# A hybrid network on one core: the SSD stage without GpSimd, its 1/rms in two parts

## Chip, core, metric

One core of one Trainium2 chip runs the whole program: TensorE (PE), VectorE (DVE), ScalarE (ACT), GpSimd (POOL) and the DMA queues that SyncE (SP) feeds. The metric is the device time of one execution in microseconds; lower is better.

## What is computed

The network takes 512 tokens of width 1024 through a gated delta rule with a conv feed-forward, a chunked attention with another, an S5 mixer with a squared-ReLU MLP, a Mamba-2 mixer (SSD) with a second MLP, and a final norm. The change lies in the SSD mixer and in the first lines of the two MLPs. The reference of the mixer, cut:

```python
def _ssd_mixer(h, w_in, conv_w, conv_b, dt_bias, a_log, d, norm_g, w_out):
    z, xbc, dt_raw = jnp.split(h @ w_in, [M2_D_INNER, M2_D_INNER + M2_CONV_DIM], axis=-1)
    xbc = jax.nn.silu(_causal_dwconv(xbc, conv_w) + conv_b)
    xs, b_in, c_in = jnp.split(xbc, [M2_D_INNER, M2_D_INNER + G * N], axis=-1)
    ...
    y_diag = jnp.einsum('bcgls,bgrcls,bcsgrp->bclgrp', cb, l_mat, xdt)
    ...
    y = y_diag + y_off + xs * d.astype(f32).reshape(G, R, 1)
    y = y.reshape(bsz, L, M2_D_INNER) * jax.nn.silu(z.astype(f32))
    yg = y.reshape(bsz, L, G, M2_D_INNER // G)
    yg = yg * lax.rsqrt(jnp.mean(yg * yg, axis=-1, keepdims=True) + NORM_EPS)
    return (yg.reshape(bsz, L, M2_D_INNER) * norm_g).astype(h.dtype) @ w_out
# second_block: x = x + g1 * mixer(modulate(rmsnorm(x)))
```

The norm `yg` is taken over each of four groups of 512 channels, for every token.

## The kernel before

Features lie on the 128 partitions, the 512 tokens on the free axis. The residual is eight tiles `h` of 128x512. A product with a weight is made of three: weight and activation are each split into a high and a low part (`hi` by ACT at L305, `lo` by DVE at L306, activations in `split`), and `mm_ch` (L347 to L349) issues hi·hi, hi·lo and lo·hi. So a projection to 128 columns of the 1024 inputs is 24 matmuls, one from the 512 channels of a group 12. The PSUM banks are dealt out in lanes (`mm` for projections, `sm` for small products, `y`).

The mixer goes through its four groups. Written `I(g,i)`, group g has ten in-projections: 0 and 1 give B and C, 2 to 5 the four x tiles (these six get a causal convolution, three DVE operations at L607, and a SiLU), 6 to 9 the four gates z. `ssd_core(g, step)` is C0: the product C·B, masked, and B transposed; C1: x to token order and scaled (L1800, L1803), exp of the decay differences D, times C·B (L1835); C2 and C3: the chunk states and E's loads; C4 to C7: one y tile each, plus t, times z, split, squared and summed; C8: column sums (L1879), mean square (L1881), a Newton 1/sqrt on 128x4 (L420 to L427), a diagonal of it (`dg`, L1885), ones·dg (L1887) and the copy r (L1889). D of the next group is loaded from DRAM and 32 subtractions (L1757) made of it in C5 and C7. `O(g,i)`, the out-projections by pairs, are made from y without 1/rms; `ssd_out` multiplies by gate and r (L1895) and adds to `h` (L1898).

The order of the work is a list written out by hand in `ssd_seq`; a recording layer then interleaves what follows within each engine. C8 of a group stands behind I4 of the next:

```python
q += [I[4]] + ([("core", g - 1, 8)] if g else []) + [C[0], I[5], I[6], C[1]]
```

At the start of the stage four projections are already in PSUM (`heads`, made in `finish` of the stage before) and have to be multiplied by 1/rms of the input (`rb`, L1770) before their banks are free. `ssd_gates` follows (dt, its loads and small products). After the last group `finish` closes the next norm with L492.

POOL does the additions to `h` (27 of 32), the products D times C·B (28 of 32), and y plus t, y times z, the state decay and most sums of squares of the first three groups.

Of the kernel before, what the change touches and what calls it, by code (L numbers as in the profile page):

```python
# [224 lines left out]
class Net:  # L225
# [1359 lines left out]
    def mlp(self, l):  # L1585
# [3 lines left out]
        with ExitStack() as es:  # L1589
# [35 lines left out]
    def ssd(self, l):  # L1625
        nc = self.nc
        with ExitStack() as es:
            g1 = es.enter_context(self.tc.tile_pool(name="ssd1", bufs=1))
            wk = es.enter_context(self.tc.tile_pool(name="ssd", bufs=2))
            op = es.enter_context(self.tc.tile_pool(name="ssdo", bufs=6))  # L1630
            self.sg, self.swk, self.sop = g1, wk, op

# [9 lines left out]
            self.S = [dict(x={}, z={}, o={}, xd={}, prev={}) for _ in range(4)]  # L1642
            heads, self.heads = self.heads, None
            self.set_lanes(mm=(4, 0, 1, 2), sm=(3, 5, 6, 7))
            for name, g, i in self.ssd_seq():
                if name in ("in", "z") and heads:
                    self.ssd_in(g, i, heads.pop(0), self.shc["ssd"][:, i:i + 1])
                    if not heads:
                        self.ssd_gates()
                        self.set_lanes(mm=(0, 1, 2), sm=(3, 4, 5), y=(6, 7))  # L1650
                elif name == "in":
                    w = self.next("m2_in", 128)
                    ps = self.mmp()
                    self.mm_ch(ps, w, 0, self.xs())
                    self.ssd_in(g, i, ps)
                elif name == "out":
                    if (g, i) == (3, 0):
                        self.set_lanes(mm=(0, 1, 2, 6, 7), sm=(3, 4, 5))
                    w = self.next("m2_out", 256)
                    pss = [self.mmp() for _ in range(2)]  # L1660
                    for j in range(2):
                        self.mm_ch(pss[j], w, j * P, [self.S[g]["o"][k] for k in range(4)])
                    if (g, i) == (3, 0):
                        self.ssd_core(3, 8)
                    for j in range(2):
# [6 lines left out]
    sbufs = dict(x=5, z=4, xd=4, B=1, E=3, CB=1, Bt=1, prev=3, r=1)  # L1672

    def ssd_seq(self):

        q = [("in", 0, i) for i in range(4)]
        for g in range(4):
            I = [("in", g, i) for i in range(10)]
            N = [("in", g + 1, i) for i in range(4)]
            C = [("core", g, i) for i in range(9)]  # L1680
            O = [("out", g - 1, i) for i in range(4)]
            q += [I[4]] + ([("core", g - 1, 8)] if g else []) + [C[0], I[5], I[6], C[1]]
            if g == 0:
                q += [I[7], C[2], I[8], C[3], I[9], C[4], N[0], C[5], N[1], C[6], N[2], C[7], N[3]]
            elif g < 3:
                q += [I[7], C[2], O[0], C[3], I[8], O[1], C[4], I[9], N[0], C[5], O[2], N[1], O[3], C[6],
                      N[2], C[7], N[3]]
            else:
                q += [O[0], C[2], O[1], C[3], I[7], O[2], C[4], I[8], C[5], O[3], C[6], I[9], C[7]]
        return q + [("out", 3, i) for i in range(4)]  # L1690

    def ssd_plan(self):
        for name, g, i in self.ssd_seq():
            if name == "in":
                self.queue.append(("m2_in", 10 * g + i))
            elif name == "out":
                self.queue.append(("m2_out", 4 * g + i))
# [4 lines left out]
    def ssd_gates(self):  # L1702
# [42 lines left out]
        for hf in range(2):  # L1745
            self.ssd_rows(0, hf)

    def ssd_rows(self, g, hf):

        nc = self.nc  # L1750
        h0 = 8 * g + 4 * hf
        self.S[g]["D", hf] = d = self.stile("D", 4)
        nc.sync.dma_start(out=d, in_=self.srow[0, h0:h0 + 4, :].partition_broadcast(P))
        for r in range(4):
            for c in range(4):
                x = d[:, r, c * P:(c + 1) * P]
                nc.vector.tensor_scalar(out=x, in0=x, scalar1=self.acs[:, h0 + r, c:c + 1], scalar2=0.0,  # L1757
                                        op0=ALU.subtract, op1=ALU.min)

    def ssd_in(self, g, i, ps, shift=None):  # L1760
# [21 lines left out]
    def ssd_core(self, g, step):  # L1782
# [22 lines left out]
        def state(c):  # L1805
# [5 lines left out]
            else:  # L1811
                t = self.stile("t")
                gp.tensor_tensor(out=r3(t, 8), in0=r3(S["prev"][c], 8), in1=hb(self.decb, c), op=ALU.mult)
# [13 lines left out]
        elif step == 1:  # L1827
            to_tok(0)
            to_tok(1)
            for hf in range(2):  # L1830
                d = S["D", hf]
                s.activation(d, d, AF.Exp)
                for r in range(4):
                    e = v if g == 0 and r % 2 else gp
                    e.tensor_tensor(out=d[:, r, :], in0=d[:, r, :], in1=S["CB"], op=ALU.mult)  # L1835
# [13 lines left out]
        elif step < 8:  # L1849
# [9 lines left out]
            e = v if g == 3 else gp  # L1859
# [8 lines left out]
            if 0 < j < (3 if g == 3 else 4):  # L1868
                (v if j == 3 else e).tensor_tensor(out=sq, in0=S["sq"], in1=sq, op=ALU.add)
            S["sqs"], S["sq"] = ([S["sq"], sq] if (g, j) == (3, 3) else [sq]), sq  # L1870
            if j % 2 == 1 and g < 3:
                self.ssd_rows(g + 1, j // 2)
        else:

            ps = self.smp()
            sqs = S["sqs"]
            for c in range(4):
                for x in sqs:
                    pe.matmul(ps[:, c:c + 1], x[:, cs(c)], self.ones[:, 0:1], start=x is sqs[0], stop=x is sqs[-1])  # L1879
# [3 lines left out]
            dg = self.stile("t")  # L1883
# [3 lines left out]
            pe.matmul(ps, self.ones, dg, start=True, stop=True)  # L1887
            S["r"] = self.stile("r")
            s.copy(S["r"], ps)  # L1889

    def ssd_out(self, g, ot, ps, gate):

        nc = self.nc
        t = self.stile("t")
# [4 lines left out]
        if g == 3:  # L1899
            self.done(ot)  # L1900
# [150 lines left out]
```

## Time and profile before

| | us |
|---|---|
| median of 3 runs | 2775.3 (2773.09 to 2775.48) |
| the profiled execution, its own time | 2773.28 |
| its span in the profile | 2771.5 |
| the SSD stage, 1998.0 to 2404.5 | 406.5 |
| mean granted TensorE clock of the span | 0.982 |

The profile is one execution. Times in it run from the start of the span. A busy time is that of an engine's instructions; a wait is the idle time of an engine in front of an instruction with what released it; the granted clock is the share of TensorE's full speed that it was given in the stretch, where 1.0 stands for 2.4 GHz and 0.5 for 1.2 GHz.

### The profile page before, as it was taken

The numbers are of one execution on the slowest core, as the hardware profiler recorded it, in microseconds if no ns is written. First come the engines' busy times: TensorE is split into PE (matmuls) and PEld (weight loads), VectorE is DVE, ScalarE is ACT, GpSimd is POOL, SyncE is SP. The second block draws the span as 40 slices with busy tenths as digits, with TensorE's granted clock in tenths as the row PEclk, the third lists the DMA queues.
The fourth block names the chain that finished last, engine by engine and source line by source line (L and its number), as shares of the span: only waits on it lengthen the run. The fifth ranks groups of instructions, "written<-read, shape, count | busy, mean of one in ns | idle before, by whom it ended". The sixth has DMA issues, their size and how long they took to land. (4 is left out here: it accounts for less than half of the span.)

```text
span 2771.5 us, 36994 instructions
## 1 busy us (share of the span) xinstructions
PE 2638.3 (95%) x14002; PEld 2121.9 (77%) x14002; DVE 1932.4 (70%) x3332; ACT 1178.4 (43%) x1867; POOL 514.9 (19%) x448
## 2 busy tenths in 40 slices
PE   8899999999999999979998999999999898999998
PEld 6677778888786868767877778888767787778886
DVE  7878889797938689998577565444677767844343
ACT  7555454242437554234264352332554433533232
POOL 0211010000112210446642110000224333300001
PEclk9999999999999999989999999999999999999999
DMA  5323247676733335354449434333333332232322
GB/s 180 121 81 83 75 137 235 214 239 203 232 114 94 109 109 162 99 156 133 145 143 268 130 118 127 98 99 92 93 118 101 114 114 80 71 96 93 99 96 72
DMA packets 172706, 356.34 MB, mean 129 GB/s; under 512 B 44048, under 2 KB 81648, under 8 KB 171504
## 3 DMA queue, kind: packets, MB, share of 16 engines
q1 hardware_dynamic: 163056, 349.78, 40.3%
q10 hardware_dynamic: 9472, 4.20, 0.5%
q8 instruction: 110, 1.80, 0.3%
q14 instruction: 68, 0.56, 0.1%
HBM read 324.00 MB, written 25.72 MB: 126 GB/s over the span
## 5 line engine op out<-in xcount | busy, mean ns | idle before, releaser
L305 ACT CAST hi<-raw 128x1024 fp32r<-128x1024 f32 (+1 forms) x416 | 432.4, 1041 | 863.3 <-PE mm L348 750.2
L347 PE MATMUL mm<-xh,hi 128*128 128x512 f32 x1824 | 739.6, 406 | 23.7 <-ACT hi L305 10.5
L349 PE MATMUL mm<-xh,lo 128*128 128x512 f32 x1824 | 727.2, 399 | 1.1 <-DVE lo L306 1.1
L348 PE MATMUL mm<-xl,hi 128*128 128x512 f32 x1824 | 724.1, 397 | 0.8 <-DVE xl L441 0.8
L306 DVE TENSOR_TENSOR lo<-raw,hi 128x1024 fp32r<-128x1024 f32 (+1 forms) x416 | 529.8, 1274 | 250.8 <-ACT hi L305 243.4
L347 PEld LDWEIGHTS mm<-xh,hi 128*128 128x128 f32 x1824 | 348.5, 191 | 103.3 <-ACT hi L305 14.6
L349 PEld LDWEIGHTS mm<-xh,lo 128*128 128x128 f32 x1824 | 347.2, 190 | 81.1 <-DVE lo L306 3.4
L348 PEld LDWEIGHTS mm<-xl,hi 128*128 128x128 f32 x1824 | 348.2, 191 | 76.8 <-issue 3.2
L347 PE MATMUL mm<-ah,hi 128*128 128x512 f32 x864 | 339.9, 394 | 0.9 <-ACT hi L305 0.7
L349 PE MATMUL mm<-ah,lo 128*128 128x512 f32 x864 | 338.5, 392 | 1.9 <-DVE lo L306 1.9
L348 PE MATMUL mm<-al,hi 128*128 128x512 f32 x864 | 338.3, 392 | 0.0
L481 POOL TENSOR_TENSOR nsq<-nsq,nsq 128x512 f32<-128x512 f32 x54 | 92.6, 1722 | 1161.7 <-ACT nsq L479 764.7
L607 DVE SCALAR_TENSOR_TENSOR cv<-cvr,par,cv 128x511 f32<-128x511 f32 (+2 forms) x248 | 204.8, 826 | 1.5 <-ACT cv L603 0.4
L349 PEld LDWEIGHTS mm<-ah,lo 128*128 128x128 f32 x864 | 163.3, 189 | 37.8 <-DVE lo L306 3.6
L347 PEld LDWEIGHTS mm<-ah,hi 128*128 128x128 f32 x864 | 163.5, 189 | 37.3 <-ACT hi L305 2.5
L348 PEld LDWEIGHTS mm<-al,hi 128*128 128x128 f32 x864 | 163.4, 189 | 34.3 <-DVE al L566 0.4
L579 DVE SCALAR_TENSOR_TENSOR h<-mm,mods,h 128x512 f32<-128x512 f32 x64 | 48.1, 751 | 195.6 <-PE mm L349 195.6
L1142 DVE SCALAR_TENSOR_TENSOR acc<-araw,condt,acc 128x1024 f32<-128x1024 f32 x93 | 121.5, 1307 | 10.1 <-DMA araw<-ada 9.9
L577 DVE TENSOR_TENSOR h<-mm,h 128x512 f32<-128x512 f32 x112 | 76.4, 685 | 65.9 <-PE mm L349 65.5
L347 PE MATMUL mm<-soh,hi 128*128 128x512 f32 x256 | 101.0, 398 | 2.3 <-ACT soh L565 2.3
L348 PE MATMUL mm<-sol,hi 128*128 128x512 f32 x256 | 100.5, 393 | 0.3 <-DVE sol L566 0.3
L349 PE MATMUL mm<-soh,lo 128*128 128x512 f32 x256 | 100.2, 392 | 0.5 <-DVE lo L306 0.5
(530 smaller groups left out, 3946.7 us busy)
## 6 DMA issues: line engine op xcount, KB each, us to landing
raw<-mlp SPq DMA_DIRECT2D x128, 512.0 KB, 3.4
araw<-ada SPq DMA_DIRECT2D x96, 512.0 KB, 4.4
raw<-f_up SPq DMA_DIRECT2D x88, 512.0 KB, 3.9
raw<-m_in SPq DMA_DIRECT2D x40, 512.0 KB, 3.5
raw<-a_in SPq DMA_DIRECT2D x32, 512.0 KB, 4.0
raw<-f_down SPq DMA_DIRECT2D x32, 512.0 KB, 3.9
raw<-b_kv SPq DMA_DIRECT2D x16, 512.0 KB, 3.6
raw<-s_glu SPq DMA_DIRECT2D x16, 512.0 KB, 4.0
```

What stands on the lines that cost most here:

```text
L305: self.nc.scalar.copy(hi[:, :sz], raw[:, :sz])
L306: self.nc.vector.tensor_tensor(out=lo[:, :sz], in0=raw[:, :sz], in1=hi[:, :sz].bitcast(F32), op=ALU.subtract)
L347: self.nc.tensor.matmul(ps, a, xh, start=(start and k == 0), stop=False)
L348: self.nc.tensor.matmul(ps, a, xl, start=False, stop=False)
L349: self.nc.tensor.matmul(ps, b, xh, start=False, stop=(stop and k == n - 1))
L481: p.eng.tensor_tensor(out=sq, in0=p.acc[i][-1], in1=sq, op=ALU.add)
L577: nc.vector.tensor_tensor(out=self.h[ot], in0=ps, in1=self.h[ot], op=ALU.add)
L579: nc.vector.scalar_tensor_tensor(out=self.h[ot], in0=ps, scalar=g[:, ot:ot + 1], in1=self.h[ot], op0=ALU.mult, op1=ALU.add)
L607: nc.vector.scalar_tensor_tensor(out=t[:, d:], in0=ps[:, :T - d], scalar=taps[n - 1 - d], in1=t[:, d:], op0=ALU.mult, op1=ALU.add)
L1142: v.scalar_tensor_tensor(out=acc, in0=raw, scalar=cond[:, k:k + 1], in1=acc, op0=ALU.mult, op1=ALU.add)
```

## The change

1. **No POOL in the stage.** D times C·B (L1863), y plus t, y times z (L1890, L1891), the state decay (L1842) and the sums of squares (L1898) are all DVE's.
2. **y is scaled before it is split.** Four multiplications of y by r per group (L1923), then the split. The out-projections, now single, then need only `add_out`, one DVE operation with gate and `h` (L579) in the place of L1895, and the additions to `h` fall away.
3. **C8 becomes three steps.** `sum` (column sums, 1/sqrt, `dg` in one broadcast product, L1913), `rms` (ones·dg, L1917, and r) and `out` (the scaling and the split). C0, I5 and I6 stand between `sum` and `rms`, C1 and I7 between `rms` and `out`, C2 before the first O.
4. **D's load and its subtractions are apart.** The load is issued in C5 and C7 as before; the first 16 subtractions stand at the end of C7, the others behind the next projection (`tail`).
5. **The last group in another order.** I8 and I9 come early, the out-projections of group 2 stand between C4 and C7 and cover `sum`, `rms` and `out` of group 3.
6. **The first banks are emptied at once.** The four products with `rb` are the stage's first (L1652), I(0,4) goes to a fifth bank ahead of `ssd_gates`. In the MLPs too the four L1599 stand together.

Tiles: `y` gets four buffers, the split y four in the place of six.

```diff
...
-            for i, ps in enumerate(heads):
-                a = wk.tile([P, T], F32, tag="ra", name=self.nm("ra"), bufs=4)
-                v.tensor_tensor(out=a, in0=ps, in1=self.rb, op=ALU.mult)
+            ras = []
+            for ps in heads:
+                ras.append(wk.tile([P, T], F32, tag="ra", name=self.nm("ra"), bufs=4))
+                v.tensor_tensor(out=ras[-1], in0=ps, in1=self.rb, op=ALU.mult)
+            for i, a in enumerate(ras):
...
+            for ps in heads:
+                ts.append(self.stile("xd"))
+                nc.vector.tensor_tensor(out=ts[-1], in0=ps, in1=self.rb, op=ALU.mult)
...
+                    if ts:
+                        self.ssd_gates()
+                        for j, t in enumerate(ts):
+                            nc.scalar.activation(t, t, AF.Identity, bias=self.shc["ssd"][:, j:j + 1])
+                            self.ssd_in(0, j, t)
...
-                    for j in range(2):
-                        self.ssd_out(g, 2 * i + j, pss[j], self.mod[l][:, 16:24])
+                    ps = self.mmp()
+                    self.mm_ch(ps, out, (i % 2) * P, [self.S[g]["o"][k] for k in range(4)])
+                    self.add_out(ps, i, gate, last=(g == 3))
...
+            q += I(g, 4)
+            if g:
+                q += C(g - 1, "sum")
+            q += C(g, 0) + I(g, 5, 6)
+            if g:
+                q += C(g - 1, "rms")
+            q += C(g, 1) + I(g, 7)
+            if g:
+                q += C(g - 1, "out")
+            q += C(g, 2)
...
+                q += I(3, 8) + C(3, 3) + I(3, 9) + C(3, 4)
+                q += O(2, 0) + C(3, 5) + O(2, 1) + C(3, 6) + O(2, 2) + C(3, 7)
+                q += O(2, 3, 4) + C(3, "sum") + O(2, 5, 6) + C(3, "rms", "out") + O(2, 7) + O(3, *range(8))
...
-                    e = v if g == 0 and r % 2 else gp
-                    e.tensor_tensor(out=d[:, r, :], in0=d[:, r, :], in1=S["CB"], op=ALU.mult)
+                    v.tensor_tensor(out=d[:, r, :], in0=d[:, r, :], in1=S["CB"], op=ALU.mult)
...
-            e.tensor_tensor(out=y[:, P:], in0=y[:, P:], in1=t[:, P:], op=ALU.add)
-            e.tensor_tensor(out=y, in0=y, in1=S["z"][j], op=ALU.mult)
-            S["o"][j] = self.split(self.sop, y, tag="so", gain=self.p("m2_ng", 4 * g + j))
+            v.tensor_tensor(out=y[:, P:], in0=y[:, P:], in1=t[:, P:], op=ALU.add)
+            v.tensor_tensor(out=y, in0=y, in1=S["z"][j], op=ALU.mult)
+            S["y"].append(y)
+            if j % 2 == 1 and g < 3:
+                self.ssd_rows(g + 1, j // 2)
...
-            for c in range(4):
-                v.tensor_scalar(out=dg[:, cs(c)], in0=ident, scalar1=y[:, c:c + 1], scalar2=None, op0=ALU.mult)
+            S["dg"] = dg = self.stile("t")
+            v.tensor_tensor(out=r3(dg, 4), in0=ident.unsqueeze(1).to_broadcast([P, 4, P]), in1=bc(y, P), op=ALU.mult)
+        elif step == "rms":
...
+                y = S["y"][j]
+                v.tensor_tensor(out=y, in0=y, in1=S["r"], op=ALU.mult)
+                S["o"][j] = self.split(self.sop, y, tag="so", gain=self.p("m2_ng", 4 * g + j))
...
-        nc.vector.scalar_tensor_tensor(out=t, in0=ps, scalar=gate[:, ot:ot + 1], in1=self.S[g]["r"],
-                                       op0=ALU.mult, op1=ALU.mult)
-        e = nc.vector if g == 3 and ot in (1, 3, 5, 6, 7) else nc.gpsimd
-        e.tensor_tensor(out=self.h[ot], in0=self.h[ot], in1=t, op=ALU.add)
```

How this moves instructions. On **DVE at the start of the stage** (`raw` is a weight as loaded, `mm` a PSUM bank, `xd` and `t` tiles in SBUF) the order was, and is:

```order
L1770 TENSOR_TENSOR t_17832<-mm_17661,rb 128x512
L1770 TENSOR_TENSOR t_17842<-mm_17706,rb 128x512
L306 TENSOR_TENSOR lo_18045<-raw_17784,hi_18044 128x1024
L607 SCALAR_TENSOR_TENSOR cv_17835<-t_17832,par,cv_17835 128x511
L607 SCALAR_TENSOR_TENSOR cv_17845<-t_17842,par,cv_17845 128x511
L607 SCALAR_TENSOR_TENSOR cv_17835<-t_17832,par,cv_17835 128x510
L607 SCALAR_TENSOR_TENSOR cv_17845<-t_17842,par,cv_17845 128x510
L607 SCALAR_TENSOR_TENSOR cv_17835<-t_17832,par,cv_17835 128x509
L607 SCALAR_TENSOR_TENSOR cv_17845<-t_17842,par,cv_17845 128x509
L1770 TENSOR_TENSOR t_17852<-mm_17746,rb 128x512
L1770 TENSOR_TENSOR t_17862<-mm_17786,rb 128x512
L368 TENSOR_TENSOR E_17875<-y_17873,E_17874 128x256
```

```order
L306 TENSOR_TENSOR lo_17842<-raw_17744,hi_17841 128x1024
L1652 TENSOR_TENSOR xd_17833<-mm_17661,rb 128x512
L1652 TENSOR_TENSOR xd_17835<-mm_17706,rb 128x512
L1652 TENSOR_TENSOR xd_17837<-mm_17746,rb 128x512
L1652 TENSOR_TENSOR xd_17839<-mm_17786,rb 128x512
L306 TENSOR_TENSOR lo_18046<-raw_17784,hi_18045 128x1024
L368 TENSOR_TENSOR E_17875<-y_17873,E_17874 128x256
L607 SCALAR_TENSOR_TENSOR cv_17993<-xd_17833,par,cv_17993 128x511
```

All four banks are now emptied side by side, ahead of the first convolution.

On **PE between groups 2 and 3** (`mm_20193`, before, is I5 and `mm_20231` I6; `mm_20141`, after, is I5 and `mm_20179` I6; 24 matmuls each) it was, and is:

```order
L1879 MATMUL sm_20141<-ones,sq_20044 128x1 x4
L1818 MATMUL sm_20173<-C_19917,B_19797 128x128 x4
L1824 MATMUL sm_20180<-par,B_19797 128x128 x4
L347 MATMUL mm_20193<-xh_81,hi_20103 128x512
...
L349 MATMUL mm_20193<-xh_88,lo_20104 128x512
L347 MATMUL mm_20231<-xh_81,hi_20187 128x512
L348 MATMUL mm_20231<-xl_89,hi_20187 128x512
L349 MATMUL mm_20231<-xh_81,lo_20188 128x512
L1887 MATMUL sm_20169<-t_20164,ones 128x512
L347 MATMUL mm_20231<-xh_82,hi_20187 128x512
```

```order
L1908 MATMUL sm_20096<-ones,sq_19985 128x1 x4
L1847 MATMUL sm_20121<-C_19868,B_19772 128x128 x4
L1853 MATMUL sm_20128<-par,B_19772 128x128 x4
L347 MATMUL mm_20141<-xh_81,hi_20058 128x512
...
L349 MATMUL mm_20141<-xh_88,lo_20059 128x512
L347 MATMUL mm_20179<-xh_81,hi_20135 128x512
...
L349 MATMUL mm_20179<-xh_88,lo_20136 128x512
L1917 MATMUL sm_20206<-t_20119,ones 128x512
L1827 MATMUL sm_20210<-par,x_19962 128x128
L1827 MATMUL sm_20210<-par,x_20040 128x128
```

From the column sums to ones·dg PE had C0, I5 and the first three matmuls of I6; it now has C0 and the whole of I5 and I6.

On **DVE in the same place**, up to `dg` (`t_20164` before, `t_20119` after; `cv` is the convolution, `D` the decay tile):

```order
L1881 TENSOR_SCALAR ms_20146<-sm_20141 128x4
L1820 TENSOR_TENSOR CB_20178<-sm_20173,par 128x512
L425 TENSOR_TENSOR rq_20151<-rq_20149 128x4
L426 TENSOR_TENSOR rq_20151<-rq_20151,rq_20150 128x4
L427 SCALAR_TENSOR_TENSOR rq_20149<-rq_20151,rq_20149 128x4
...
L306 TENSOR_TENSOR lo_20226<-raw_20107,hi_20225 128x1024
L426 TENSOR_TENSOR rq_20151<-rq_20151,rq_20150 128x4
L427 SCALAR_TENSOR_TENSOR rq_20149<-rq_20151,rq_20149 128x4
L1885 TENSOR_SCALAR t_20164<-par,rq_20149 128x128 x4
```

```order
L427 SCALAR_TENSOR_TENSOR rq_20104<-rq_20106,rq_20104 128x4
L607 SCALAR_TENSOR_TENSOR cv_20166<-mm_20141,par,cv_20166 128x511
L425 TENSOR_TENSOR rq_20106<-rq_20104 128x4
L1863 TENSOR_TENSOR D_19983<-D_19983,CB_20126 128x512
L426 TENSOR_TENSOR rq_20106<-rq_20106,rq_20105 128x4
L607 SCALAR_TENSOR_TENSOR cv_20166<-mm_20141,par,cv_20166 128x510
L427 SCALAR_TENSOR_TENSOR rq_20104<-rq_20106,rq_20104 128x4
L1863 TENSOR_TENSOR D_19983<-D_19983,CB_20126 128x512
L1913 TENSOR_TENSOR t_20119<-par,rq_20104 128x512
```

The seven products with C·B that were POOL's now stand, with a convolution, between the steps of the 1/sqrt, and one operation makes `dg`.

## Rows read from the trace of the kernel before

**Rows 1.** The page's line of busy time, share of the span and instructions by engine

```profile
PE 2638.3 (95%) x14002; PEld 2121.9 (77%) x14002; DVE 1932.4 (70%) x3332; ACT 1178.4 (43%) x1867; POOL 514.9 (19%) x448
```

**Rows 2.** Window table of the stage; columns: start:end, us, engines' busy us, clock, DMA share, GB/s

```profile
1998.00:2404.50 406.50, 372.73 (x1839) 293.05 (x1837) 299.37 (x503) 175.57 (x217) 136.59 (x99) 0.96 0.30 99
```

**Rows 3.** Waits of PE, 1998 to 2427 us (waiter <- releaser: us, times, longest)

```profile
PE sm L1887 <- DVE t L1885: 13.9, 2, 7.0
PE sm L1798 <- ACT x L1776: 3.8, 1, 3.8
PE mm L347 <- DVE t L1770: 3.2, 1, 3.2
PE y L1857 <- DVE t L1862: 2.9, 1, 2.9
...
PE y L1854 <- DVE y L1860: 2.2, 2, 1.6
...
PE y L1854 <- DVE D L1835: 1.3, 1, 1.3
PE mm L347 <- DVE t L1895: 1.3, 1, 1.3
```

**Rows 4.** Window table of the first and last of six low-clock stretches

```profile
2001.50:2004.70 3.20, 3.16 (x8) 2.53 (x9) 2.76 (x4) 2.73 (x4) 0.00 (x0) 0.51 0.79 232
...
2395.50:2400.40 4.90, 4.14 (x10) 2.94 (x11) 4.90 (x5) 3.42 (x5) 3.14 (x3) 0.67 0.30 107
sum 24.30, PE 23.33 PEld 16.11 DVE 19.69 ACT 11.06 POOL 6.17; mean PE 3.89 PEld 2.69 DVE 3.28 ACT 1.84 POOL 1.03
```

**Rows 5.** Chain that ended last, 2290 to 2312 us (start, us, what)

```profile
2292.56 2.04 DVE D L1757 x10
...
2305.01 1.19 DVE rq L426
...
2309.87 0.17 DVE rq L427
...
2310.07 0.07 DVE t L1885
...
2311.00 1.22 PE sm L1887
```

**Rows 6.** Groups of DVE by line, 2000.7 to 2404.2 us (busy us, mean ns | idle before)

```profile
L306 DVE TENSOR_TENSOR lo<-raw,hi 128x1024 fp32r<-128x1024 f32 x53 | 76.2, 1439 | 31.5 <-ACT hi L305 30.0 <-PE y L1857 0.7
...
L425 DVE TENSOR_TENSOR rq<-rq 128x4 f32<-128x4 f32 x12 | 9.1, 758 | 0.2
...
L427 DVE SCALAR_TENSOR_TENSOR rq<-rq,rq 128x4 f32<-128x4 f32 x12 | 7.7, 640 | 0.3
L426 DVE TENSOR_TENSOR rq<-rq,rq 128x4 f32<-128x4 f32 x12 | 6.0, 498 | 0.2
L1898 DVE TENSOR_TENSOR h<-h,t 128x512 f32<-128x512 f32 x5 | 5.6, 1113 | 0.0
```

**Rows 7.** The same of POOL

```profile
L1835 POOL TENSOR_TENSOR D<-D,CB 128x512 f32<-128x512 f32 x28 | 39.3, 1435 | 36.3 <-DVE CB L1820 27.4 <-ACT D L1832 8.9
```

**Rows 8.** Timeline of DVE, two operations in a row (start us, us)

```profile
2118.34 0.68 DVE L1803 TENSOR_TENSOR xe<-sm,swend 128x512 f32<-128x512 f32 x1
2118.94 0.68 DVE L1800 TENSOR_TENSOR xd<-sm,sdt 128x512 f32<-128x512 f32 x1
```

**Rows 9.** Timeline of PE, two matmuls in a row (start us, us)

```profile
2106.12 0.39 PE L349 MATMUL mm<-xh,lo 128*128 128x512 f32 x1
2106.35 0.39 PE L347 MATMUL mm<-xh,hi 128*128 128x512 f32 x1
```

**Rows 10.** Timeline of ACT, start and end of the stage (start us, us)

```profile
2004.72 0.41 ACT L367 CAST E<-y 128x256 fp32r<-128x256 f32 x1 [0.49 <-DMA y<-m_dtw]
...
2382.14 0.58 ACT L1889 COPY r<-sm 128x512 f32<-128x512 f32 x1 [6.31 <-PE sm L1887]
```

**Rows 11.** Tile D, 2150 to 2300 us: its loads

```profile
DMA to landing us min/median/max: 6.6/6.6/6.6
```

More of the change, by code (lines that the diff above doesn't have):

```diff
@@ L1629, in ssd @@
             wk = es.enter_context(self.tc.tile_pool(name="ssd", bufs=2))
-            op = es.enter_context(self.tc.tile_pool(name="ssdo", bufs=6))
+            op = es.enter_context(self.tc.tile_pool(name="ssdo", bufs=4))
             self.sg, self.swk, self.sop = g1, wk, op
+            g1.tile([P, 16], F32, name="spad")
             def free(k):
@@ L1641, in ssd @@
             self.lend(wk, [("xd", 4)], free)
-            self.S = [dict(x={}, z={}, o={}, xd={}, prev={}) for _ in range(4)]
+            self.S = [dict(x={}, z={}, o={}, xd={}, prev={}, y=[]) for _ in range(4)]
             heads, self.heads = self.heads, None
-            self.set_lanes(mm=(4, 0, 1, 2), sm=(3, 5, 6, 7))
-            for name, g, i in self.ssd_seq():
[L1646 to L1651, printed above, removed]
+            ts = []
+            for ps in heads:
+                ts.append(self.stile("xd"))
+                nc.vector.tensor_tensor(out=ts[-1], in0=ps, in1=self.rb, op=ALU.mult)
+            self.set_lanes(mm=(4, 0, 1, 2), sm=(6, 7, 5, 3))
+            out = None
+            for name, g, i in self.ssd_seq():
+                if name == "in":
+                    if ts and (g, i) < (0, len(heads)):
+                        continue
                     w = self.next("m2_in", 128)
@@ L1658, in ssd @@
                         self.set_lanes(mm=(0, 1, 2, 6, 7), sm=(3, 4, 5))
-                    w = self.next("m2_out", 256)
-                    pss = [self.mmp() for _ in range(2)]
-                    for j in range(2):
[L1662 to L1665, printed above, removed]
-                        self.ssd_out(g, 2 * i + j, pss[j], self.mod[l][:, 16:24])
+                    if i % 2 == 0:
+                        out = self.next("m2_out", 256)
+                    ps = self.mmp()
+                    self.mm_ch(ps, out, (i % 2) * P, [self.S[g]["o"][k] for k in range(4)])
+                    self.add_out(ps, i, gate, last=(g == 3))
                 else:
@@ L1695, in ssd_plan @@
                 self.queue.append(("m2_in", 10 * g + i))
-            elif name == "out":
-                self.queue.append(("m2_out", 4 * g + i))
+            elif name == "out" and i % 2 == 0:
+                self.queue.append(("m2_out", 4 * g + i // 2))
     def stile(self, tag, n=0):
@@ L1812, in state @@
                 t = self.stile("t")
[L1813 removed]
+                v.tensor_tensor(out=r3(t, 8), in0=r3(S["prev"][c], 8), in1=hb(self.decb, c), op=ALU.mult)
                 v.tensor_tensor(out=nx, in0=ps, in1=t, op=ALU.add)
@@ L1848, in ssd_core @@
             state(2)
-        elif step < 8:
+        elif step in (4, 5, 6, 7):
             j = step - 4
@@ L1862, in ssd_core @@
             v.tensor_tensor(out=t[:, P:], in0=po[:, P:], in1=S["E"][j][:, P:], op=ALU.mult)
-            e.tensor_tensor(out=y[:, P:], in0=y[:, P:], in1=t[:, P:], op=ALU.add)
-            e.tensor_tensor(out=y, in0=y, in1=S["z"][j], op=ALU.mult)
-            S["o"][j] = self.split(self.sop, y, tag="so", gain=self.p("m2_ng", 4 * g + j))
+            v.tensor_tensor(out=y[:, P:], in0=y[:, P:], in1=t[:, P:], op=ALU.add)
[3 more added lines that the diff above has]
+                self.ssd_rows(g + 1, j // 2)
             sq = self.stile("sq")
             s.activation(sq, y, AF.Square)
[L1868 to L1873, printed above, removed]
+            if 0 < j:
+                v.tensor_tensor(out=sq, in0=S["sq"], in1=sq, op=ALU.add)
+            S["sq"] = sq
+            if j == 3 and g < 3:
+                self.ssd_exps(g + 1, 0)
+        elif step == "tail":
+            self.ssd_exps(g + 1, 1)
+        elif step == "sum":
             ps = self.smp()
-            sqs = S["sqs"]
             for c in range(4):
-                for x in sqs:
-                    pe.matmul(ps[:, c:c + 1], x[:, cs(c)], self.ones[:, 0:1], start=x is sqs[0], stop=x is sqs[-1])
+                pe.matmul(ps[:, c:c + 1], S["sq"][:, cs(c)], self.ones[:, 0:1], start=True, stop=True)
             ms = self.swk.tile([P, 4], F32, tag="ms", name=self.nm("ms"), bufs=2)
```

61 lines of the change are left out of this document (30 added, 31 removed).

## The prediction

> **What bounds the kernel now.** The page's first line comes first [rows 1]: PE is busy 95% of the span, every other engine 70% or less. So time can be won only where PE stands still or runs slowly. The window table tells how much of that lies in the stage that is changed [rows 2]: 406.5 us, of which PE is busy 372.7, so 33.8 us of idle time. The table of PE's waits says where [rows 3]: 13.9 us before ones·dg (L1887), twice 7.0, at the boundaries between groups 1 and 2 and between 2 and 3; 3.8 before a transpose (L1798) at the boundary before those; 3.2 at the start, for a PSUM bank that L1770 empties; 2.9, 2.2 and 1.3 in group 0, before y's products; 1.3 at the end, for a bank that L1895 empties. The rest are waits under 2 us. Behind each of these gaps the granted clock falls from 1.0 to about 0.5, the level of 1.2 GHz: six stretches, 24.3 us together, five at 0.50 to 0.52 and one at 0.67 [rows 4]. Half of 19.4 us and a third of 4.9 us are about 11 us lost. The most that a better order could win is thus about 33.8 + 11 = 45 us, 1.6% of the time.
>
> The chain through the last boundary shows why PE waits there [rows 5]. It is all DVE: ten of the D subtractions in 2.04 us, then the 1/sqrt, whose 128x4 steps take 1.19 us in the middle of it and 0.17 at its end. DVE's groups show that this is common: L425, four numbers per partition, 0.76 us on average [rows 6]; the lo split 1.44 us. The long ones fall where POOL works on D times C·B, 1.44 us each [rows 7].
>
> **The change, part by part.** The price of a DVE operation on 128x512 is read from two in a row: each lasts 0.68 us, but the second starts 0.60 behind the first [rows 8]. I take 0.60.
>
> *Work on DVE.* It gains 28 products with C·B, 12 y plus t, 12 times z, 8 decays, 7 sums of squares, 16 products with r and 4 broadcast products: 87 × 0.60 = 52 us. It loses 16 small diagonals at about 0.2 (3 us) and five additions to `h` (5.6 us [rows 6]). L579 replaces L1895 one for one. Net +44. Without POOL the 36 Newton steps should fall from 9.1 + 7.7 + 6.0 = 23 us [rows 6] to 36 × 0.20 = 7, the step from L427 to L1885 at the end of the chain [rows 5]: −16. The 53 lo splits, twice as many elements as 128x512, I take at 1.2 in the place of 1.44: −12. DVE then has 299 + 44 − 28 = 315 us of a stage of about 383: 82%. No longer a spectator, but below PE. Whatever it has to do late will show in PE.
>
> For prices per matmul: PE starts one every 0.23 us [rows 9], so an in-projection is 24 × 0.23 = 5.5 us, an out-projection of 12 is 2.7.
>
> *Start (3.2 us idle, 1.6 in the clock).* I4 now has a bank of its own, so the wait for L1770 goes. Next late is the dt projection, whose activations come by a DMA that the ACT cast waits for; the cast ends at 2004.72 + 0.41 = 2005.1 [rows 10]. PE stood still for 3.2 us up to 2001.5, so without that wait I4 runs from 1998.3 to 2003.8 and PE is idle about **1.5** until the cast is through. Ends: 0 if the load moves up, 3.2 if nothing is won.
>
> *Group 0 (6.4 us).* Four of the eight products with C·B were already DVE's, beside POOL's four at 1.44; eight at 0.60 on DVE are 4.8 us against 5.7, about as long. y plus t and y times z stand on DVE between the products that free the y banks. I leave a bit over half: **3.5**. Ends: 0 and 10, the 17 operations of 0.60 that are added here.
>
> *Boundary 0/1 (3.8 us and a lo split).* C1's transposes are moved behind I6 and the x tile that they waited for is ready. The lo splits of I5 and I6 now queue behind D's subtractions and the new products. I take **2.4**, plus 0.7 for `out` (below). Ends 0 and 5.
>
> *Boundaries 1/2 and 2/3 (7.5 us each).* From the mean square to `dg` DVE has C·B, five convolution steps and seven products, 13 × 0.60 = 7.8; a lo split of 1.2; 13 small operations, at most 0.20 each, partly filled in, about 2.0; `dg` 0.60: 11.6 us. PE covers that with C0 (1.1) and 11 us of I5 and I6, 12.1. But DVE comes late to the mean square: D's load is issued when C7's products release the tile and lands 6.6 us later [rows 11]; 16 subtractions (0.20 each [rows 5]: 3.3), y times z, a sum of squares, three convolution steps and a lo split follow, 7.6 in all, 14.2 us behind C7, whereas PE has passed the next two projections and is at the sum after 11 to 12.5. So DVE is some 1.8 behind and PE waits **1.4**. Then `out`: r, three products, four splits and what stands ahead (a convolution step, a product, four operations of C1, two lo splits) are 11 us; PE has C1, I7 and C2 (8 us) and needs the last split tile only three quarters into its first out-projection, 10 in all: **0.7** with what the `rms` wait lets DVE catch up. 2.1 per boundary, ends 0 and 7.5. The loads of D and of the weights keep their order on SP; D's issue still waits for C7 and the weights behind it have the slack of four pieces. Out-weights are fetched every second O: no more loads than before.
>
> *Last group (3.8 us).* `sum` and `rms` are covered by O(2,3) to O(2,6), four times 2.7 us. Behind ones·dg, O(2,7) covers 2.7 us; the copy r takes 0.58 [rows 10], a product 0.60, the splits another 1.2 before O(3,0) can begin: near 3. The last tile is later by some 1.5 us. The close of the norm (L492) still waits for POOL's last sum: 1.5. **3.0**.
>
> *In between*, where DVE at 82% holds a bank or a lo split a moment longer: **3.5**, an allowance of 0.05 us for each of some 70 such handovers. Ends 0 and 10. *Clock*: fewer and shorter gaps, so **3** of the 11 us stay; if every gap of a microsecond costs a fall, 8.
>
> Sum of what stays: 1.5 + 3.5 + 3.1 + 4.2 + 3.0 + 3.5 + 3 = 21.8. Of 45 lost us some 23 come back: 2773.3 − 23 = **2750** us, against the profiled execution's own time, which lies 2.0 below the median of the runs; I keep 2750. The front of the MLPs I cost at nothing: four products in another order, hidden under projections.
>
> The overlap of 0.08 us between two DVE operations [rows 8] carries weight, since 87 are added. The Trainium skill, "VectorE: DVE Perf Modes", section "The DRAIN you can't avoid", says that the next operation does not start until the pipe of the last has emptied (with an exception for one that nothing holds), and advises to minimise the count of operations. By that each added one would cost its whole 0.68: 7 us more for DVE, some 1 us at each boundary, and 2754. The two rows bear it out for waiting operations only.
>
> **Rivals.** *DVE becomes the bound.* For it: 82% on average, and at the boundaries the 1/sqrt stands behind seven products, in order. Against it: the long Newton steps go. If DVE comes to the mean square 5 us behind PE in the place of 1.8, each of three boundaries loses 3.2 more and group 0 about 2.5: +12, **2762**. From where it is 2 us late each further microsecond shows.
>
> *Slower: the split behind r is not covered.* Before, the out-projections needed no r; now four times per program every O waits for r, four products, and four splits, 11 us of DVE in order. If DVE arrives 10 us late at ones·dg (or the stretch of its operations is not POOL's doing and stays), the cover of 10 us is spent: some 8 us at each of the four places. 4 × 8 = 32 more than forecast, **2782**. It decides from about 7 us at each place. Against it: PE waits at ones·dg for the same queue, so both start from there together.
>
> *No change.* The removed waits come back elsewhere, as waits for weights (hi by ACT) or a longer clock fall: within 5 us of **2773**. Against it: ACT is busy 176 of 406 us and DMA 0.30 [rows 2]. That the change would not do what it says can be left out: the order of the instructions shows the moves.
>
> **How the numbers follow.** Forecast 62%, spread 2737 (8 us of waits stay) to 2757; DVE the bound 22%; slower 8%; no change 8%. A measurement of this kernel tells about 0.2%, 5.5 us, from nothing. Faster: the first two and a little of the last, 0.84; same 0.08; slower 0.08. The range is 2736 to 2766: it takes in the first case and nearly all of the second.
>
> **What would show it.** Right: PE's waits for L1887's successor L1917 fall from 7.0 to under 2 each; L425 to L427 take 0.16 to 0.2 everywhere; the lo split 1.2; POOL has only the norm's sums left; DVE is busy 305 to 325 us of some 384. The first rival: waits of PE at L1917 or on y over 3 us each. The second: long waits of the first O of a group for the split tiles. The prediction is wrong if Newton steps stay at 0.5 us and more without POOL, or if the granted clock falls as often as before.

## The result, and the profile after

The changed kernel takes 2742.33 us (median of 4 runs, 2741.86 to 2746.59) against 2775.27: ratio 0.9884, 95% interval 0.9872 to 0.9896. That is 33 us less; 25 less were forecast, and the time lies inside the range. The profiled execution was the slowest of the four, 2746.59 us with a span of 2744.8; the one of before had 2773.28. It also comes to the stage 5.6 us later, by work that lies ahead of it. So stretches are compared here from one mark to another: from the first square sums (L492) of SSD's input norm to those of the final norm. That was 777.2 us (1980.1 to 2757.3) and is 744.9 (1985.7 to 2730.6): 32.3 less, 28.8 in the stage itself and 3.5 in the MLP behind it. I call it **the marked stretch** from here on.

The page's line by engine [rows 1], now:

```profile
PE 2629.9 (96%) x13994; PEld 2116.7 (77%) x13994; DVE 1929.6 (70%) x3398; ACT 1180.1 (43%) x1867; POOL 385.7 (14%) x355
```

DVE does 66 instructions more and is busy 3 us less. The window table of the stage [rows 2], group by group and the whole (us, busy PE, PEld, DVE, ACT, POOL, granted clock, DMA share, GB/s):

```profile
2003.60:2381.30 377.70, 368.52 (x1835) 289.92 (x1834) 300.17 (x572) 177.37 (x219) 8.13 (x6) 0.98 0.33 108
2003.60:2099.00 95.40, 86.29 (x432) 65.95 (x431) 77.73 (x174) 55.27 (x68) 0.00 (x0) 0.94 0.35 122
2099.00:2196.00 97.00, 96.99 (x481) 77.04 (x481) 74.43 (x142) 42.70 (x51) 0.00 (x0) 0.99 0.37 117
2196.00:2290.00 94.00, 93.97 (x474) 75.18 (x473) 71.55 (x137) 40.57 (x49) 0.00 (x0) 1.00 0.35 116
2290.00:2381.30 91.30, 91.27 (x452) 71.76 (x451) 76.47 (x122) 38.83 (x54) 8.13 (x6) 1.00 0.25 79
```

The stage fell from 406.5 to 377.7 us. From 2099 on PE does not stand still at all: 0.07 us in 282. All that is left lies in the first 95 us, and the table of PE's waits in the stage [rows 3] is short:

```profile
PE mm L347 <- DVE cv L607: 4.4, 1, 4.4
PE sm L347 <- issue: 1.4, 1, 1.4
PE sm L1908 <- DVE sq L1898: 1.3, 1, 1.3
PE sm L1744 <- ACT t L1741: 1.0, 1, 1.0
PE sm L1827 <- ACT Bt L1855: 0.9, 1, 0.9
```

The 13.9 us in front of ones·dg are gone, and nothing took their place. Of the six low-clock stretches [rows 4] one is left, behind the first of these waits:

```profile
2087.00:2100.70 13.70, 9.18 (x25) 7.12 (x26) 13.70 (x43) 7.81 (x8) 0.00 (x0) 0.50 0.23 76
```

Half of its 9.18 busy microseconds, 4.6, are lost. Groups of DVE in the stage [rows 6]:

```profile
L306 DVE TENSOR_TENSOR lo<-raw,hi 128x1024 fp32r<-128x1024 f32 x54 | 66.9, 1239 | 33.4 <-ACT hi L305 32.5
...
L1863 DVE TENSOR_TENSOR D<-D,CB 128x512 f32<-128x512 f32 x32 | 21.0, 684 | 0.0
...
L426 DVE TENSOR_TENSOR rq<-rq,rq 128x4 f32<-128x4 f32 x12 | 1.9, 156 | 0.1
L427 DVE SCALAR_TENSOR_TENSOR rq<-rq,rq 128x4 f32<-128x4 f32 x12 | 1.9, 156 | 0.1
L425 DVE TENSOR_TENSOR rq<-rq 128x4 f32<-128x4 f32 x12 | 1.9, 155 | 0.1
```

The 36 Newton steps fell from 22.8 to 5.7 us, the lo split from 1.44 to 1.24. The products with C·B, 1.44 on POOL, are 0.68 here. Eight in a row took 4.90 us, which is a start every 0.60:

```profile
2056.53 4.90 DVE L1863 TENSOR_TENSOR D<-D,CB 128x512 f32<-128x512 f32 x8
```

So DVE's busy time in the stage is 300 us, as before, with all of POOL's work in it but the additions to `h`, which fell away.

The boundary between groups 2 and 3 as DVE's timeline shows it (start, us, operation), the counterpart of the chain [rows 5], and then the end of it on PE:

```profile
2287.06 0.16 DVE L1910 TENSOR_SCALAR ms<-sm 128x4 f32<-128x4 f32 x1 [0.32 <-PE sm L1908]
...
2295.35 0.16 DVE L427 SCALAR_TENSOR_TENSOR rq<-rq,rq 128x4 f32<-128x4 f32 x1
...
2298.16 0.68 DVE L1913 TENSOR_TENSOR t<-par,rq 128x512 f32<-128x512 f32 x1
```

```profile
2299.50 1.02 PE L1917 MATMUL sm<-t,ones 128*128 128x512 f32 x2
```

DVE waits for PE's column sums here, not the other way. From the mean square to the end of `dg` it takes 11.8 us, 0.8 of them spent waiting for PE's product C·B (11.6 were counted, with no wait), and `dg` lies ready 0.7 us before PE comes to it. Between groups 1 and 2 it is the same. Between 0 and 1 PE still waits for DVE, 1.3 us for a sum of squares.

### The profile page after: what moved, and what is told of

The parts are those of the page before. It is cut to its first block, busy times and chain, and to the rows that moved or that the text cites. A ratio compares the mean times of both kernels' runs of the same rounds, so it can differ in the third digit from the quotient of the medians.

```text
span 2744.8 us, 36915 instructions
## 1 busy us (share of the span) xinstructions
PE 2629.9 (96%) x13994; PEld 2116.7 (77%) x13994; DVE 1929.6 (70%) x3398; ACT 1180.1 (43%) x1867; POOL 385.7 (14%) x355
## 5 line engine op out<-in xcount | busy, mean ns | idle before, releaser
L306 DVE TENSOR_TENSOR lo<-raw,hi 128x1024 fp32r<-128x1024 f32 (+1 forms) x416 | 519.1, 1248 | 251.9 <-ACT hi L305 246.0
L579 DVE SCALAR_TENSOR_TENSOR h<-mm,mods,h 128x512 f32<-128x512 f32 x96 | 71.9, 749 | 205.5 <-PE mm L349 205.2
L347 PE MATMUL mm<-soh,hi 128*128 128x512 f32 x256 | 100.8, 400 | 2.7 <-ACT soh L565 2.7
```

Of the source, the lines that this page charges most:

```text
L306: self.nc.vector.tensor_tensor(out=lo[:, :sz], in0=raw[:, :sz], in1=hi[:, :sz].bitcast(F32), op=ALU.subtract)
L347: self.nc.tensor.matmul(ps, a, xh, start=(start and k == 0), stop=False)
L579: nc.vector.scalar_tensor_tensor(out=self.h[ot], in0=ps, scalar=g[:, ot:ot + 1], in1=self.h[ot], op0=ALU.mult, op1=ALU.add)
```

## Experiments

Every run shared its runs of before with others on one chip. The changed kernel itself, run once more beside the last ones, stands for the scatter:

> The changed kernel itself, beside the next two on one chip: ratio to before 0.987 to 0.990, the 4.4 us wait at the end of group 0 again, no wait over 1 us from group 1 on.

Ratio 0.989 (0.9871 to 0.9909); marked stretch 743.7 us (744.9 in the first profile), stage 377.1 (377.7), wait at the end of group 0 3.8 us (4.4). A difference of 1 us tells nothing, then. The marked stretch also holds the MLP behind the stage, which took 351.9 to 353.3 us in the three profiles with the old order of its first lines and 348.7 to 350.9 in the eleven with the new one. So the length of the stage is given beside the marked stretch. Each of these two lengths comes from one profile per run.

**Was it the cover, or POOL?** Two things had changed at the boundaries at once: more matmuls stand in front of ones·dg, and POOL no longer works beside the 1/sqrt.

```diff
-            q += [I[4]] + ([("core", g - 1, 8)] if g else []) + [C[0], I[5], I[6], C[1]]
+            q += [I[4]] + ([("core", g - 1, 8)] if g else []) + [C[0], I[5], I[6]] + R + [C[1]]
```

(R is ones·dg and r alone, as step 9.)

> The kernel before with one thing changed: ones·dg and r are a step of their own behind I6, so 48 matmuls of projections stand between the column sums and ones·dg in the place of 27; POOL keeps all its work. Theory 'cover' (the gain came because more of TensorE's work stands in front of ones·dg): the two waits of 7.0 us go to under 1 each, with part of the clock falls behind them, time 2755 to 2762. Theory 'POOL' (the gain came because POOL no longer stretches DVE's operations): the 1/sqrt stays stretched, 21 matmuls more are 4.8 us, so 2 us of each wait stay and the lateness comes out behind, at r's readers: 2765 to 2773.

2770.2 us against 2776.18, ratio 0.9983 (0.9971 to 0.9995), the range of theory 'POOL'; marked stretch 772.1, 5.1 less than before (stage 402.4, 4.1 less). Its waits and its Newton steps:

```profile
PE sm L1800 <- ACT x L1778: 7.5, 3, 4.3
PE sm L1890 <- DVE t L1887: 6.8, 2, 3.4
```

```profile
L425 DVE TENSOR_TENSOR rq<-rq 128x4 f32<-128x4 f32 x12 | 9.1, 759 | 0.2
```

The 21 matmuls more shorten each wait from 7.0 to 3.4, and 3.7 us of that come back as waits of C1's transposes. Cover alone is worth 5 of the 32 us. The other half of the pair takes POOL away and leaves the written order:

```diff
-                    e = v if g == 0 and r % 2 else gp
-                    e.tensor_tensor(out=d[:, r, :], in0=d[:, r, :], in1=S["CB"], op=ALU.mult)
+                    v.tensor_tensor(out=d[:, r, :], in0=d[:, r, :], in1=S["CB"], op=ALU.mult)
...
-        e = nc.vector if g == 3 and ot in (1, 3, 5, 6, 7) else nc.gpsimd
+        e = nc.vector
```

(and in the same way L1813, L1863, L1864, L1869.)

> The kernel before with POOL's work of the SSD stage on DVE and nothing else; the written order is that of before, but the recording layer, which now finds DVE's queue longer, puts ones·dg behind 53 matmuls instead of 27. Theory 'POOL': the 1/sqrt's steps fall from 0.5-0.76 us to 0.16-0.2, lo splits to 1.2, waits before ones·dg under 1 us, 2745 to 2757. Theory 'cover': the waits go too, for the 53 matmuls, but DVE has some 60 us more work and only the layer's placement helps; what is gained is the two waits and little else, 2757 to 2765. Third possibility, DVE becomes the bound: over 2775.

2760.72 us, ratio 0.9939 (0.9927 to 0.9951); marked stretch 760.4, 16.8 less (stage 389.2, 17.3 less). No wait for ones·dg is left, L425 takes 0.16 us; but others stand in the table:

```profile
PE y L1853 <- DVE y L1859: 7.9, 1, 7.9
PE mm L349 <- DVE lo L306: 5.1, 2, 3.8
PE mm L347 <- DVE t L1770: 3.2, 1, 3.2
PE sm L1878 <- DVE sq L1868: 3.2, 1, 3.2
```

Half of the gain thus comes with the old written order, though not from POOL's absence alone: 53 matmuls stand in front of ones·dg here, 27 before. Against `before_cover`, with 48 in front and POOL at work, it is 11.7 us less. The time lies in the range of theory 'cover', while the steps went as 'POOL' said, and the waits were to go by both. So this run doesn't decide between them; the next one is the sharper:

```diff
-                    v.tensor_tensor(out=d[:, r, :], in0=d[:, r, :], in1=S["CB"], op=ALU.mult)
+                    e = v if g == 0 and r % 2 else gp
+                    e.tensor_tensor(out=d[:, r, :], in0=d[:, r, :], in1=S["CB"], op=ALU.mult)
```

> The changed kernel with 28 of the 32 products D times C·B back on POOL, as before the change. Theory 'cover': ones·dg has the same 48 matmuls in front, so its waits stay under 1 us; time within 4 us of the changed kernel's 2742, whatever the length of the 1/sqrt's steps. Theory 'POOL': the steps are stretched again to 0.5 us and more, dg comes 3 to 5 us behind the cover at each of three boundaries, and the clock falls behind the gaps: 2752 to 2762.

2761.86 us, ratio 0.9943 (0.9931 to 0.9956); marked stretch 759.9, 15.0 more than the changed kernel (stage 391.7, 14.0 more). 28 products on POOL, with all the cover in place, are enough to bring the waits and the long steps back:

```profile
PE sm L1918 <- DVE t L1914: 7.0, 3, 3.4
PE sm L1827 <- ACT x L1805: 4.9, 2, 2.4
```

```profile
L426 DVE TENSOR_TENSOR rq<-rq,rq 128x4 f32<-128x4 f32 x12 | 8.3, 690 | 0.4
```

With 28 operations fewer DVE is busy longer, 310.1 us in the place of 300.2. This decides for the theory 'POOL' at the boundaries. The Trainium skill, "SBUF — State Buffer", section "SBUF: two separate sides", says that a DVE operation with two SBUF inputs and a GpSimd operation share a port pair that one of them holds for its whole length. The trace agrees: before, at the boundaries 1/2 and 2/3, five of nine Newton steps took 1.18 to 1.22 us in the midst of POOL's products (1.26 to 1.31 us each), and 0.15 to 0.16 behind the last of them. It was not the small operations alone. A lo split took 2.34 us beside an addition of POOL, 1.22 without, whereas a convolution step, which reads PSUM, kept its 0.74 in the midst of POOL's products:

```profile
2142.42 1.27 POOL L1898 TENSOR_TENSOR h<-h,t 128x512 f32<-128x512 f32 x1 [1.39 <-DVE t L1895]
2142.43 2.34 DVE L306 TENSOR_TENSOR lo<-raw,hi 128x1024 fp32r<-128x1024 f32 x1
...
2301.16 0.73 DVE L607 SCALAR_TENSOR_TENSOR cv<-mm,par,cv 128x509 f32<-128x509 f32 x1
...
2302.52 1.22 DVE L427 SCALAR_TENSOR_TENSOR rq<-rq,rq 128x4 f32<-128x4 f32 x1
```

(all four of the kernel before)

**The other parts, each undone in the changed kernel.** First the last group's order:

```diff
-                q += O(2, 3, 4) + C(3, "sum") + O(2, 5, 6) + C(3, "rms", "out") + O(2, 7) + O(3, *range(8))
+                q += O(2, *range(3, 8)) + C(3, "sum", "rms", "out") + O(3, *range(8))
```

> The changed kernel with all of group 2's out-projections ahead of the last group's sums, so that nothing covers the last 1/rms. Both theories: column sums to dg takes 13 small operations of 0.2, 0.6 for dg, then r 0.6, products and splits 2 to 3 us until the first out-projection can begin: a gap of 6 to 8 us in two pieces and 2 us of low clock, 2750 to 2753. Rival, that the end needs no cover because the layer fills it: under 2 us, 2742 to 2744.

2752.28 us, ratio 0.9907 (0.9890 to 0.9924), which overlaps the changed kernel's; marked stretch 753.4, 8.5 more (stage 386.8, 9.1 more). The gap comes in the two pieces expected:

```profile
PE sm L1917 <- DVE t L1913: 4.2, 1, 4.2
PE mm L347 <- ACT soh L568: 2.2, 1, 2.2
```

Then r in front of the split:

```diff
-                v.tensor_tensor(out=y, in0=y, in1=S["r"], op=ALU.mult)
...
-                    self.add_out(ps, i, gate, last=(g == 3))
+                    nc.vector.scalar_tensor_tensor(out=t, in0=ps, scalar=gate[:, i:i + 1], in1=self.S[g]["r"],
+                                                   op0=ALU.mult, op1=ALU.mult)
+                    nc.vector.tensor_tensor(out=self.h[i], in0=self.h[i], in1=t, op=ALU.add)
```

(the split stands in C4 to C7 again, and the tiles of y and of its split have as many buffers as before.)

> The changed kernel with y split without r as before, and r applied to the out-projections (two DVE operations each in the place of one); sums, ones times dg and all orders stay. DVE gets 32 additions and loses 16 products: 16 x 0.6 = 10 us more, at 83% of the stage. Theory 'the rest of the gain is order and POOL's absence': no wait hangs on r in front of the split, so 0 to 4 us slower: 0.9884 to 0.990. Rival 'scaling y first is where the rest came from': 5 to 12 us slower, 0.990 to 0.9925. Rival, that the split behind r cost something: faster.

2750.72 us, ratio 0.9907 (0.9894 to 0.9921), which touches the changed kernel's; marked stretch 753.0, 8.1 more (stage 385.2, 7.5 more): the range of the rival 'scaling y first'. DVE is busy 312.7 us of the stage instead of 300.2, and the waits show where it is late, at the column sums and in the close of the norm:

```profile
PE sm L1913 <- DVE sq L1903: 4.4, 1, 4.4
...
PE mm L348 <- DVE z L441: 2.9, 1, 2.9
```

The start:

```diff
+                    if ts:
+                        self.ssd_gates()
                     w = self.next("m2_in", 128)
                     ps = self.mmp()
                     self.mm_ch(ps, w, 0, self.xs())
                     if ts:
-                        self.ssd_gates()
```

> The changed kernel with the dt projection ahead of I(0,4) again, the four first products still together: TensorE has nothing to do from the end of the heads until the cast of the dt weights, about the 5.5 us of I4 less 2 us for the four products: 3 to 6 us slower than the changed kernel, ratio 0.9895 to 0.9905. Rival, that I4's place does not matter since the small products of the gates wait for DVE and ACT anyway and I4 can fill those gaps: within 1.5 us, 0.988 to 0.989.

Ratio 0.9896 (0.9879 to 0.9913), which settles nothing; the marked stretch is 747.5, 2.6 to 3.8 more, but the stage 378.8, only 1.1 to 1.7 more. The rest lies in the MLP behind it. One new wait stands in the table:

```profile
PE sm L347 <- ACT E L367: 3.3, 1, 3.3
```

It takes the place of the 1.4 and 1.0 at the start of the changed kernel, 0.9 more in all. The place of I4 is thus worth about 1 us, no more than the scatter, which is the rival's case.

And D's subtractions. In `before_no_pool` DVE stood 7.3 us for D's load, and y's operations behind it; that is the 7.9 us above.

```diff
                 self.ssd_rows(g + 1, j // 2)
+                self.ssd_exps(g + 1, j // 2)
```

(and the two other places of the subtractions fall away.)

> The changed kernel with the subtractions on D right behind their load again, in C5 and C7. In the profile of 'before_no_pool' DVE stood 7.3 us for D's load in group 0, with y's operations queued behind, and TensorE 7.9 us for y. Theory 'the split of load and subtraction is needed once DVE does it all': the same gap comes back in group 0, 6 to 8 us in the place of the 4.4 us wait, and smaller ones in groups 1 and 2; 4 to 12 us slower than the changed kernel, ratio 0.9905 to 0.993. Rival, that the other changes of order already keep y ahead: within 2 us, 0.988 to 0.9897.

Ratio 0.9891 (0.9872 to 0.9910), marked stretch 745.8, stage 377.6: the rival's case. This part of the change cost and brought nothing that shows here.

**What is left at the end of group 0.** The 4.4 us are put down to a convolution on DVE. Followed back, engine by engine (timelines of PE, DVE, ACT and SP of the changed kernel; in brackets what ended the idle time):

```profile
2089.31 0.77 PE L347 MATMUL mm<-xh,hi 128*128 128x512 f32 x1 [4.43 <-DVE cv L607]
```

```profile
2085.57 0.75 DVE L607 SCALAR_TENSOR_TENSOR cv<-mm,par,cv 128x511 f32<-128x511 f32 x1 [7.00 <-ACT cv L605]
```

```profile
2083.81 1.05 ACT L305 CAST hi<-raw 128x1024 fp32r<-128x1024 f32 x1 [8.21 <-DMA raw<-m_in]
```

```profile
2069.01 1.22 DVE L306 TENSOR_TENSOR lo<-raw,hi 128x1024 fp32r<-128x1024 f32 x1
...
2070.25 2.25 SPq L295 DMA_DIRECT2D raw<-m_in  x1
DMA to landing us min/median/max: 13.5/13.5/13.5
```

A weight lands late; ACT waits for it with the convolution queued behind. Its load was issued at 2070.25, as soon as an older weight's split was done (2070.23), and landed 13.5 us later (the last line, of this load alone), when the cast began. When the next two runs were planned I took another load for it, the one issued at 2078.80 behind D's load; that one is for the next cast, at 2093.00. Two ways to have it earlier were tried, D's loads (and then E's too) from POOL's idle queue, and a fourth buffer for loaded weights in this stage.

```diff
-        self.nc.sync.dma_start(out=d, in_=self.srow[0, h0:h0 + 4, :].partition_broadcast(P))
+        self.nc.gpsimd.dma_start(out=d, in_=self.srow[0, h0:h0 + 4, :].partition_broadcast(P))
```

> The changed kernel with D's loads issued by POOL, which has nothing else to do there, in the place of SP. In the changed kernel's profile TensorE stands 4.4 us at the end of group 0: it waits for a convolution on DVE, DVE for its first part on ACT, ACT for a weight, and that weight's load was issued behind D's load, which waited for C7. Theory 'queue': with D's load out of SP the weight is issued some 2 us earlier, the 4.4 us shrink to 1 to 2 and the clock falls less: 3 to 6 us faster than the changed kernel, ratio to before 0.986 to 0.988. Rival 'weight buffers': the weight's load waits for its buffer (three of them) anyway, nothing changes: 0.9884. Rival 'slower loads': loads from POOL land later than 6.6 us, D's subtractions are late, the mean square too: over 0.990.

> The same with E's loads from POOL too, so that SP has nothing but weights in the stage. Theory 'queue': as the run before or 1 to 2 us better, since E's loads too wait for buffers in front of weights: 0.985 to 0.987. Rival 'weight buffers': 0.9884. Rival 'slower loads': over 0.990.

With D alone 2750.36 us, ratio 0.9904 (0.9889 to 0.9919), marked stretch 750.8, 6 more than the changed kernel (stage 382.7, 5 more); with E too 2743.83, 0.9882 (0.9865 to 0.9899), 743.8 (stage 377.2), no change. The gap of the first only moved, and grew:

```profile
PE sm L1847 <- ACT C L1805: 6.3, 1, 6.3
```

Counted from the first mark (1983.0 here, 1985.7 in the changed kernel) the weight's load was issued after 88.0 us and its cast began after 100.8, against 84.6 and 98.1: no earlier. It had not been D's load that held it. With E's loads from POOL as well it was issued after 88.0 again, but landed in 8.4 us in the place of 13.5, and the cast began after 96.5. So a part of the late landing seems to come from the loads in front of it on SP; PE then waited 2.2 and 2.1 us elsewhere, and nothing was won. The other way:

```diff
+        if self.rawx is not None and name.startswith("m2") and q % 4 == 3:
+            raw = self.rawx.tile([P, 1024], F32, tag="rawx", name=self.nm("raw"), bufs=1)
+        else:
+            raw = self.wpool.tile([P, 1024], F32, tag="raw", name=self.nm("raw"))
```

> The changed kernel with a fourth buffer for weights as loaded, in the SSD stage alone, so that each weight's load is issued one piece earlier, ahead of D's and E's loads that it stood behind. Theory 'weights late' (the gap at the end of group 0 is a weight that lands late, the convolution on DVE only the messenger): the 4.4 us go to under 1, the two waits of 1.3 and 0.9 behind it too, and the clock no longer falls there: 8 to 10 us faster than the changed kernel, 0.985 to 0.9865. Rival 'DVE is the bound of group 0': DVE's queue is as long as before, the gap stays within 1.5 us of what it was: 0.988 to 0.989.

> The fourth weight buffer and D's and E's loads issued by POOL. Theory 'weights late': as the run before, within 2 us of it: 0.9845 to 0.9865. Rival, that loads from POOL's queue take longer (D 10 us to land in the place of 6.7) and are late now that nothing else is: 3 to 6 us slower than the run before.

2739.09 us, ratio 0.9858 (0.9842 to 0.9875), and 2739.82, 0.9865 (0.9850 to 0.9880), beside 2744.45 of the changed kernel on the same chip. The marked stretch is 740.2 and 737.4 (743.7), the stage 372.0 and 369.2 (377.1). The stage of the first:

```profile
2006.20:2378.20 372.00, 365.85 (x1836) 288.01 (x1835) 300.28 (x572) 177.34 (x220) 8.11 (x6) 1.00 0.34 109
```

The wait of 4.4 us is gone, the clock stays at 1.0, with DVE just as busy: DVE was the messenger. The cast that began 98.1 us after the first mark begins after 90.3. The gain is 3.5 us in the marked stretch and 5.1 in the stage where 8 to 10 were expected: lo splits (2.2 us) and the sums (1.5 us) still make PE wait. By its median it is the fastest kernel here; its interval and the changed kernel's overlap. So the weight was held by its buffer: a buffer more brings the cast forward by 7.8 us, D's load out of the way does not.

## Why the prediction was right

The bound was read rightly: of 33.8 us of standing still and some 11 of low clock, 9.2 and 4.6 are left. By its length the stage fell by 28.8 us (24.6 less idle, 4.2 less busy), where 23 were forecast. The other 3.5 lie in the MLP behind it, which was costed at nothing. That term may be wrong by some 3 us, the difference of the means with the old and the new order there; but no run undoes the MLPs' order alone, and the first MLP's stretch (356.6 to 359.4 us in all profiles) shows nothing of it. Some 1.7 of the 3.5 are the clock, which stood at 0.81 and 0.71 for 7 us behind the wait for L1598 before, and at 1.00 behind L1599 after. The direction held, and so did the signs that were named: Newton steps of 0.16 us, lo splits of 1.24, no wait at L1917, DVE at about 80% of the stage (79; 82 was forecast). Term by term, what was to stay and what stayed:

| place | before | forecast | after |
|---|---|---|---|
| start | 3.2 | 1.5 | 1.4 + 1.0 |
| group 0 | 6.8 | 3.5 | 4.4 |
| boundary 0/1 | 4.9 | 3.1 | 1.3 + 0.9 |
| boundaries 1/2, 2/3 | 15.1 | 4.2 | 0 |
| last group | 3.8 | 3.0 | 0 |
| in between | | 3.5 | 0 |
| low clock | 11 | 3 | 4.6 |

By the table 13.6 us stay where 21.8 were forecast. Too large were the boundaries 1/2 and 2/3 by 4.2, the allowance in between by 3.5, the last group by 3.0 and the boundary 0/1 by 0.9. The start, group 0 and the clock were too small by 0.9, 0.9 and 1.6 and hide a part of that.

At the boundaries the count of DVE's work up to `dg` was right (11.8 against 11.6), but not that DVE comes 1.8 us late to the mean square. The step that was mis-sized is D's load, taken at 6.6 us from issue to landing:

```profile
DMA to landing us min/median/max: 4.7/4.7/4.7
```

(tile D, 2150 to 2300 us, after. The landing is told for the load between groups 1 and 2; between 2 and 3 the first subtraction begins as far behind the issue.) The work behind it took 7.7 us (7.6 counted), so DVE was ready 12.3 us behind the issue and not 14.2, and PE's sums came after 12.6: DVE waits 0.3 us for PE. Why the load landed sooner stays open. `out` cost nothing. In the last group nothing stayed of the 3.0; that it needs its cover is seen in the run with the end bare; why L492 no longer waits for POOL's last sum (1.7 before) was not followed up. The allowance for what an 82% busy DVE holds up in between was not needed: from group 1 on, PE stands still for 0.07 us in 282. And DVE's own total came out 15 us under the 315 of the sum, which had left other operations at the length that POOL gave them: the 128 subtractions on D alone fell from 34.2 to 26.8 us.

What the forecast did not say is what each part does alone. At the boundaries it used both, a cover of 12.1 us and small operations at 0.20. The runs tell them apart. With POOL at work the cover brings 5 us. Behind the same cover POOL's absence brings 11.7 in the old order (`before_no_pool` against `before_cover`) and 15 in the new one (`after_cb_pool`). The end's order brings some 8.5 and r in front of the split 8, the start about 1. These do not add up to 32, since they hide one another; the broadcast product for `dg`, the single out-projections and the order in the MLPs were not tested alone. The wait at the end of group 0 stayed for another reason than the forecast gave (y's operations on DVE): a weight's buffer. I had written that the weights have the slack of four pieces; with three buffers for loaded weights they have less.

The rival 'DVE becomes the bound' is seen in `after_r_behind`: 12.5 us more of DVE work and 8 us more of time. So the changed kernel stands not far from that point: 0.7 us of slack at `dg`. The rule of the Trainium skill on the pipe that empties ("VectorE: DVE Perf Modes", section "The DRAIN you can't avoid"), by which each added operation would cost 0.68, did not come into play: the eight products in a row start 0.60 apart, which is the rule's exception for operations that nothing holds. What the split of D's load and its subtractions was for stays open; undone, it changed nothing. The MLPs, costed at nothing, keep their one wait, for L1599 (2.8 and 2.2 us; for L1598, before, 2.8 and 2.5).

## What to carry to other kernels

An engine that is idle for two thirds of a stage (POOL was busy 136.6 us of 406.5) isn't free help if its work lengthens the operations of the one that the critical path runs through. Look for small operations whose mean time is several times their shortest, and see what runs beside them. A wait put down to an engine is followed back through that engine's queue before the engine is blamed: here it ended twice at a load.

## What was not expected of the hardware

A 128x4 operation on DVE took up to 0.76 us on average and up to 1.25 beside POOL's 128x512 products, and 0.16 alone. The mean of the 128x1024 split hides the same loss (1.44 and 1.24), since most splits had no such neighbour: 2.33 to 2.36 us beside an addition of POOL, 1.22 without. So what is lost is some 1.0 to 1.1 us, a little under the length of one POOL operation (1.26 to 1.31), whatever the size of DVE's own, and a row of small dependent operations pays it at every step. Convolution steps that read PSUM lost nothing (0.74). And loads issued by POOL's queue took longer. With D's and E's loads there, D's had a median of 10.2 us from issue to landing in the stretch around group 0, in the place of 6.7 from SP; over the whole stage it was 6.8 against 5.2.
